# Sixteen more expert blocks multiplied ahead of the expert loop, and the first gates of it read from SBUF

## The chip, the core and the metric

The kernel runs on one core of one Trainium2 chip. The core has five engines that run beside each other, each in the order of its own queue: TensorE (PE, with the weight loads shown as PEld), VectorE (DVE), ScalarE (ACT), GpSimd (POOL) and SyncE (SP). SP issues nearly all plain DMA transfers, and POOL issues the gathers of table rows by index. The metric is the time of one execution in microseconds (us), lower is better.

## The reference

One step of a one-layer decoder for 512 prompt tokens and 64 sample tokens: a combined projection, retention, dilated attention, a mix of both, a layer norm, then a mixture of 16384 one-row experts (PEER), and a second layer norm. The change touches the experts alone:

```python
def block(xb):
    q = (xb @ w_q).reshape(PEER_BLOCK, H_PEER, 2, DK_PEER // 2)
    s = jnp.einsum('thsc,hskc->thsk', q, sub_keys).astype(jnp.float32)
    sv, si = lax.top_k(s, TOPK_PEER)
    ...
    e = i0 * N_KEYS + i1
    g = jax.nn.softmax(cv, axis=-1)
    a = jax.nn.gelu(jnp.einsum('td,thkd->thk', xb, u_tab[e]), approximate=False)
    return jnp.einsum('thk,thkd->td', (g * a).astype(xb.dtype), v_tab[e])
```

Each token picks 128 experts (8 heads of 16). An expert is a row of `peer_u` (dotted with the token, through gelu) and a row of `peer_v` (added with the weight g * a).

## The kernel before

**Two ways through the experts.** For 384 prompt tokens (TD = 3 tiles of 128) the kernel multiplies all 16384 experts densely, in 128 blocks of 128 experts, with a gate that is zero where a token did not pick an expert. For the last 128 prompt tokens and the 64 sample tokens it gathers the picked rows from memory: one indirect DMA brings one row of 1024 numbers for each of 128 partitions (a tile `row`, 512 KB), and VectorE dots it (`dot`, L1120) or adds it (`add`, L1129).

**A dense block has two parts.** `u_part(i)` (L1419) loads 512 KB of `uT` into `wraw`, splits it into a high and a low half (`whi` by ACT L1424, `wlo` by POOL L1425), makes 24 matmuls of 128x384 into a bank `tr`, and ACT's gelu makes the tile `act` (L1430). `v_part(i)` (L1558) loads 512 KB of `v`, splits it on ACT (L315) and DVE (L316), multiplies `act` by the gates to `wt` (DVE L1565), splits that into `wh` (ACT L315) and `wl` (DVE L316), and `products` makes 18 matmuls of 128x512 that add up in six banks through all 128 blocks. Both parts take their buffers from the same rings: three of `wraw`, four of `whi`, four of `wlo`, three of `wh`, four of `act`.

**The gates.** `spread(t)` (L1472) turns the picks of token tile t into gates: for each 32 tokens a tile `stage` of 128x(128x32) numbers is filled by matmuls of one-hot tiles (L1500) and copies on ACT (L1501), and stored to a DRAM tensor `gateD[b]`, 2 MB each, 12 in all (L1505). `stage` has one buffer under the tag `xh` and one under `xl`. In the loop, `gates(i)` (L1578) reads the gates of eight blocks back into a tile `gt`, in 12 DMAs of 128 KB, one from each `gateD`; its buffers are those of `stage`.

**Blocks ahead.** For blocks whose number modulo 8 is below `PG`, `u_part` runs ahead of the loop (`u_ahead`, L1435): 16 of them behind the last projection, 24 between the pieces of `spread`, the rest behind it (L1513). Their `act` goes to DRAM (`actD`, L1439), and the loop loads it back (L1592). With PG = 3 these are 48 of the 128 blocks.

**The loop** (L1585) takes block i's `act` (loaded or made by `u_part`) and then the products of block i - 1. For each block `advance` (L1139) lets some gathers through, behind a copy `pace` on POOL that waits for the block's `act`: three for a block that still has its `u_part`, 1.5 for one ahead, on average. The first step of that stream also finishes the sample tokens: `finish` (L1525) loads a tile `x1`, multiplies and adds it on POOL (L1529, L1530), makes `pz` on DVE, normalises, multiplies and adds once more, half on DVE and half on POOL (L1538, L1539), and stores the result (L1540).

**The order.** The program is not run as written: a scheduler puts the instructions of each engine in an order of its own by estimated times, and each engine then keeps to it. SP's queue is one such order too: a DMA whose buffer is not free, or whose source is not written, holds back all that SP issues after it.

Of the kernel before, what the change touches and what calls it, by code (L numbers as in the profile page):

```python
# [8 lines left out]
F32 = mybir.dt.float32  # L9
# [4 lines left out]
AF = mybir.ActivationFunctionType  # L14
# [15 lines left out]
NVEC = VEC_G[3]  # L30
DKS = 128.0 ** -0.5
MINF = -3.0e38
PG = 3
AHEAD = 1
HEAD = 16
ON_ACT = 1
# [188 lines left out]
def body(tc, I, O, dbg=None):  # L225
    nc = tc.nc
    PE, DVE, ACT, POOL, SP = nc.tensor, nc.vector, nc.scalar, nc.gpsimd, nc.sync
# [20 lines left out]
    XA = pool("xa")  # L248
# [269 lines left out]
    for g in range(NG):  # L518
        for o in range(VEC_G[g], VEC_G[g + 1], 512):
# [3 lines left out]
            t = A.tile([8, 512], F32, name="vt", tag="vt", bufs=2)  # L523
# [441 lines left out]
    G2, t = s4k("G2s"), s4k("l1s")  # L965
# [503 lines left out]
    TB = 32  # L1469
    gateD = [DR.tile([128, 128, TB], F32, name=f"gate{b}") for b in range(ND // TB)]  # L1470

    def spread(t):  # L1472
        i01 = C.tile([128, 2, 128], F32, name="i01", tag="i01", bufs=2)
        g = C.tile([128, 128], F32, name="gw", tag="gw", bufs=2)
        route(C, 8, sv[t], si[t], i01, g)
        pt = tr_ps()
        for z, x in enumerate((i01[:, 0], i01[:, 1], g)):
            PE.transpose(pt[:, 128 * z:128 * z + 128], x, ident)
        tT = C.tile([128, 4, 128], F32, name="tT", tag="tT", bufs=2)
        ACT.activation(tT[:, 0:3, :], pt[:, 0:384].rearrange("p (z t) -> p z t", z=3), AF.Copy)  # L1480
        ACT.activation(tT[:, 3, :], pt[:, 256:384], AF.Copy, scale=-1.0)
        for b in range(128 // TB):
            stage = XA.tile([128, 128, TB], F32, name="stage", tag=("xh", "xl")[b % 2], bufs=1)
            for q in range(TB // 4):
                o = TB * b + 4 * q
                oh1 = C2.tile([128, 4, 128], F32, name="oh1", tag="oh1", bufs=3)
                oh0 = C2.tile([128, 4, 128], F32, name="oh0", tag="oh0", bufs=3)
                sh = [128, 4, 128]
                DVE.tensor_tensor(oh1, iota_p[:, None, :].to_broadcast(sh), tT[:, 1, o:o + 4, None].to_broadcast(sh), op=OP.is_equal)
                ps = ac_ps()  # L1490
                for j in range(4):
                    col = lambda z: tT[:, z, o + j:o + j + 1]
                    if j < ON_ACT:

                        ACT.activation(oh0[:, j, :], iota, AF.Abs, bias=col(0), scale=-1.0)
                        ACT.activation(oh0[:, j, :], oh0[:, j, :], AF.Relu, bias=col(2), scale=col(3))
                    else:
                        E, num = (POOL, iota) if j < ON_ACT + ON_POOL[q % 2] else (DVE, iota_p)
                        E.tensor_scalar(oh0[:, j, :], num, col(0), col(2), op0=OP.is_equal, op1=OP.mult)
                    PE.matmul(ps[:, 128 * j:128 * j + 128], oh1[:, j, :], oh0[:, j, :], start=True, stop=True)  # L1500
                ACT.activation(stage[:, :, 4 * q:4 * q + 4].rearrange("p i t -> p t i"), c4(ps), AF.Copy)  # L1501
                if q % 4 == 3:
                    u_ahead(AHEAD)
                    advance(GX, stage[:, 0, :])
            SP.dma_start(gateD[128 * t // TB + b], stage)  # L1505

    u_ahead(HEAD)
    for t in range(TD):
# [69 lines left out]
    def gates(i):  # L1578
        gt = XA.tile([128, ND // TB, IG, TB], F32, name="gt", tag=("xh", "xl")[i // IG % 2], bufs=1)
        for b in range(ND // TB):  # L1580
            SP.dma_start(gt[:, b], gateD[b][:, i:i + IG, :])
        return gt

    prev, gt_next, due, last = None, gates(0), 0.0, []
    for i in range(128):  # L1585
        if i % IG == 0:
            gt = gt_next
# [48 lines left out]
```

## Time and profile before

| | before |
|---|---|
| median of 3 runs | 2478.74 us (2473.35 to 2484.56) |
| the profiled execution | 2482.92 us, of which 2480.9 us from its first to its last instruction (the span) |
| mean granted TensorE clock | 0.941 of full speed |
| busy: PE, PEld, DVE, ACT, POOL | 90%, 76%, 71%, 41%, 47% |
| expert loop, from 1580.06 to 2440.20 us | 860.14 us, PE busy 842.05 us |

Times in the trace are counted from the start of the span. A busy share is a mean over stages with different limits, so it is read by stage; `idle before <-releaser` in a row is how long the engine had waited before that instruction, and which instruction's end let it go.

### The profile page before, as it was taken

Reading aid. Unit: us, or ns where it says so; the run is one execution under the profiler, and the core shown is the slowest. Engines: PE = TensorE matmul, PEld = TensorE weight load, DVE = VectorE, ACT = ScalarE, POOL = GpSimd, SP = SyncE. Lnnn points to the kernel's source line nnn. Section 1 sums busy time; section 2 is a strip of 40 time slices with the busy share of each in tenths; the row PEclk is TensorE's granted clock in tenths of the full one; section 3 lists DMA queues with packets and bytes.
Section 4 is the critical chain, followed back from the end, with each engine's and each line's share of the span. In section 5 each row is a group of like instructions: output and inputs, shape, how many; then the busy total and the mean of one; then the engine's idle time right before and its main releaser. Section 6 shows DMA issues by size and latency. Waiting matters only on the chain.

```text
span 2480.9 us, 35644 instructions
## 1 busy us (share of the span) xinstructions
PE 2236.0 (90%) x12729; PEld 1894.0 (76%) x12729; DVE 1762.8 (71%) x3069; ACT 1006.6 (41%) x1662; POOL 1161.4 (47%) x942
## 2 busy tenths in 40 slices
PE   7899999969899996899789994899999999999995
PEld 4885666647777874899789994788888888888884
DVE  3464112355678788779999994797887888888865
ACT  2452122334455462233358893333333333333342
POOL 0022011043026545224565563677677767777742
PEclk7899999989899996999989997899999999999998
DMA  8786786476788996486767779599889989999841
GB/s 294 265 289 218 275 292 220 164 209 218 240 317 292 330 356 230 139 281 218 272 226 276 280 253 314 201 351 342 307 320 327 333 310 350 327 337 332 312 154 51
DMA packets 222494, 671.38 MB, mean 271 GB/s; under 512 B 27307, under 2 KB 80299, under 8 KB 218827
## 3 DMA queue, kind: packets, MB, share of 16 engines
q1 hardware_dynamic: 162016, 448.32, 52.5%
q0 software_dynamic: 59904, 220.62, 24.7%
q8 instruction: 100, 1.64, 0.3%
q14 instruction: 78, 0.64, 0.1%
q10 hardware_dynamic: 396, 0.16, 0.0%
HBM read 614.38 MB, written 112.40 MB: 293 GB/s over the span
## 4 chain that ended last, share of the span: by engine, by line
PE 50%; DVE 19%; DMA 15%; issue 7%; POOL 5%; ACT 3%; SPq 1%; POOLq 0%; DVEq 0%; ACTq 0%
PE mm L423 7%; PE mm L425 6%; PE mm L424 6%; PE tr L425 4%; PE tr L423 3%; PE tr L424 3%; DMA row<-in_u_dram,e 3%; PE ac L748 2%; POOL row L1111 2%; PE ac L423 2%; PE ac L424 2%; DVE ys L1129 2%; PE ac L425 2%; DVE wlo L316 2%; DMA row<-in_v_dram,e 2%
## 5 line engine op out<-in xcount | busy, mean ns | idle before, releaser
L316 DVE TENSOR_TENSOR wlo<-wraw,whi 128x1024 fp32r<-128x1024 f32 x304 | 420.3, 1387 | 259.6 <-ACT whi L315 235.4
L315 ACT ACTIVATE whi<-wraw 128x1024 fp32r<-128x1024 f32 x304 | 319.9, 1057 | 468.9 <-PE mm L424 165.4
L1425 POOL TENSOR_TENSOR wlo<-wraw,whi 128x1024 fp32r<-128x1024 f32 x128 | 331.2, 2588 | 144.5 <-ACT whi L1424 134.4
L423 PE MATMUL tr<-x,whi 128*128 128x384 f32 x1024 | 351.6, 343 | 15.7 <-ACT act L1430 13.1
L425 PE MATMUL tr<-x,wlo 128*128 128x384 f32 x1024 | 351.2, 343 | 8.4 <-POOL wlo L1425 8.2
L424 PE MATMUL tr<-x,whi 128*128 128x384 f32 x1024 | 350.3, 342 | 0.0
L1111 POOL DMA_INDIRECT row<-in_u_dram,e x192 | 253.2, 1319 | 145.4 <-DVE row L1120 111.6
L1111 POOL DMA_INDIRECT row<-in_v_dram,e x192 | 246.4, 1283 | 159.3 <-DVE y L1129 56.4
L423 PEld LDWEIGHTS tr<-x,whi 128*128 128x128 f32 x1024 | 196.5, 192 | 21.9 <-ACT act L1430 14.2
L425 PEld LDWEIGHTS tr<-x,wlo 128*128 128x128 f32 x1024 | 195.6, 191 | 10.8 <-POOL wlo L1425 9.7
L424 PEld LDWEIGHTS tr<-x,whi 128*128 128x128 f32 x1024 | 196.1, 191 | 3.6
L1129 DVE SCALAR_TENSOR_TENSOR y<-row,acts,y 128x1024 f32<-128x1024 f32 x127 | 189.3, 1490 | 12.6 <-DMA row<-in_v_dram,e 11.5
L1120 DVE SCALAR_TENSOR_TENSOR row<-row,h2g 128x1024 f32<-128x1024 f32 x128 | 172.6, 1363 | 29.5 <-DMA row<-in_u_dram,e 28.9
L1424 ACT ACTIVATE whi<-wraw 128x1024 fp32r<-128x1024 f32 x128 | 134.7, 1052 | 99.5 <-PE ac L425 31.0
L423 PE MATMUL mm<-xh,whi 128*128 128x512 f32 x384 | 154.3, 402 | 0.1
L424 PE MATMUL ac<-wlo,wh 128*128 128x512 f32 x384 | 153.9, 401 | 0.0
L423 PE MATMUL ac<-whi,wh 128*128 128x512 f32 x384 | 153.3, 402 | 0.0
L424 PE MATMUL mm<-xl,whi 128*128 128x512 f32 x384 | 152.7, 398 | 0.0
L425 PE MATMUL mm<-xh,wlo 128*128 128x512 f32 x384 | 152.3, 397 | 0.0
L315 ACT ACTIVATE wh<-wt 128x384 fp32r<-128x384 f32 x128 | 67.0, 524 | 202.2 <-DVE wt L1565 190.7
L425 PE MATMUL ac<-whi,wl 128*128 128x512 f32 x384 | 144.7, 395 | 0.0
L423 PE MATMUL mm<-whi,xh 128*128 128x256 f32 x448 | 133.1, 299 | 9.3 <-DVE gr L1359 5.4
(410 smaller groups left out, 5337.5 us busy)
## 6 DMA issues: line engine op xcount, KB each, us to landing
wraw<-in_uT_dram SPq DMA_DIRECT2D x128, 512.0 KB
wraw<-in_v_dram SPq DMA_DIRECT2D x128, 512.0 KB
out_dram<-in_cache_dram SPq DMA_DIRECT2D x64, 508.0 KB
wraw<-in_w_ada_dram SPq DMA_DIRECT2D x48, 512.0 KB
gate<-stage SPq DMA_DIRECT2D x12, 2048.0 KB
gt<-gate SPq DMA_DIRECT2D x192, 128.0 KB
kt<-in_kc_dram POOLq DMA_DIRECT2D x32, 588.0 KB
svt<-in_vc_dram SPq DMA_DIRECT2D x72, 256.0 KB
```

What stands on the lines that cost most here:

```text
L315: ACT.activation(hi, src, AF.Copy)
L316: return DVE.tensor_tensor(lo, src, fv(hi), op=OP.subtract).ins
L423: PE.matmul(ps, a[0], b[0], start=first, stop=False)
L424: PE.matmul(ps, a[0], b[1], start=False, stop=False)
L425: PE.matmul(ps, a[1], b[0], start=False, stop=last)
L748: PE.matmul(banks[bank][32 * p:32 * p + 32, a - 512 * bank:e - 512 * bank], qz[:, g, p, b2, :], kt[b2][:, a:e], start=b2 == 0, stop=b2 == 1)
L1111: POOL.indirect_dma_start(out=r, out_offset=None, in_=I[table], in_offset=bass.IndirectOffsetOnAxis(ap=e[:, j:j + 1], axis=0))
L1120: DVE.scalar_tensor_tensor(u, u, 1.0, h2, op0=OP.mult, op1=OP.mult, accum_out=a[:, j:j + 1])
L1129: DVE.scalar_tensor_tensor(y, v, a[:, j:j + 1], y, op0=OP.mult, op1=OP.add)
L1424: ACT.activation(uh, u, AF.Copy)
L1425: POOL.tensor_tensor(ul, u, fv(uh), op=OP.subtract)
```

## The change

`PG` becomes 4, so 64 blocks are multiplied ahead. The number between the pieces of `spread` stays as it was; the 16 more are issued by the `u_ahead(128)` behind the last spread tile. In the loop, 64 blocks and not 80 have a `u_part`, and 64 and not 48 load `act` from DRAM. The first eight blocks' gates of the last 32 tokens are copied by ACT from the tile `stage` that still holds them; the other eleven pieces of that first `gt` come from DRAM as before. The lines behind the change move by 2 (from L1472) or 11 (from L1584).

```diff
-PG = 3
+PG = 4
...
+    stages = {}
+
     def spread(t):
...
             SP.dma_start(gateD[128 * t // TB + b], stage)
+            stages[128 * t // TB + b] = stage
...
-    prev, gt_next, due, last = None, gates(0), 0.0, []
+    def first_gates():
+
+        gt = XA.tile([128, ND // TB, IG, TB], F32, name="gt", tag="xh", bufs=1)
+        for b in range(ND // TB - 1):
+            SP.dma_start(gt[:, b], gateD[b][:, 0:IG, :])
+        ACT.activation(gt[:, ND // TB - 1], stages[ND // TB - 1][:, 0:IG, :], AF.Copy)
+        return gt
+
+    prev, gt_next, due, last = None, first_gates(), 0.0, []
```

The order of the engines moves with it. On TensorE, between the last one-hot matmul of `spread` and the first product, there stood 35 matmuls of `u_part` (`tr<-x`) and there stand 371 now: the rest of one part and 15 whole ones, 14 parts more than before. Three other engines show what surrounds them.

POOL, from its last one-hot tile of `spread` on, before (`wlo` belongs to a `u_part`, `pace` and `row` to the gathers, `x` and `pz` to `finish`):

```order
L1499 TENSOR_SCALAR oh_13701<-kc_iota,tT 128x128
L1425 TENSOR_TENSOR wlo<-wraw,whi 128x1024
L1143 COPY pace<-act 1x1
L1111 DMA row<-in_u_dram,e_8277 128x1024
L1143 COPY pace<-act 1x1
L1111 DMA row<-in_u_dram,e_8277 128x1024 x2
L1143 COPY pace<-act 1x1
L1111 DMA row<-in_u_dram,e_8277 128x1024
L1425 TENSOR_TENSOR wlo<-wraw,whi 128x1024
```

and in the changed kernel:

```order
L1501 TENSOR_SCALAR oh_13717<-kc_iota,tT 128x128
L1425 TENSOR_TENSOR wlo<-wraw,whi 128x1024 x8
L1532 TENSOR_TENSOR x_22032<-x_22032,l1ga 128x1024
L1533 TENSOR_TENSOR x_22032<-x_22032,l1ba 128x1024
L1425 TENSOR_TENSOR wlo<-wraw,whi 128x1024 x7
L1143 COPY pace<-act 1x1
L1532 TENSOR_TENSOR x_14720<-x_14720,l1ga 64x1024
L1111 DMA row<-in_u_dram,e_8277 128x1024
```

The gathers of the last prompt tokens now begin behind fifteen `wlo`, and the first of the `x` tiles stands between the eighth and the ninth of these.

SP, a little behind the store of the last `stage`, before (`x` is for `finish`, `gate_10675` is the last of the 12 gate tensors and `gate_10664` the first; the first row of `gt` is the last piece for blocks 0 to 7, those after it are for blocks 8 to 15):

```order
L1528 DMA x_14160<-xnD 64x1024
L1528 DMA x_20745<-xnD 128x1024
L1561 DMA wraw<-in_v_dram 128x1024
L1421 DMA wraw<-in_uT_dram 128x1024
L1581 DMA gt<-gate_10675 128x256
L1581 DMA gt<-gate_10664 128x256
L1581 DMA gt<-gate_10665 128x256
```

and in the changed kernel (`gate_10680` is the first gate tensor, `act_9169` an `actD`; all `gt` rows are for blocks 8 to 15):

```order
L1531 DMA x_14720<-xnD 64x1024
L1531 DMA x_21345<-xnD 128x1024
L1421 DMA wraw<-in_uT_dram 128x1024
L1439 DMA act_9169<-act 128x384
L1421 DMA wraw<-in_uT_dram 128x1024
L1584 DMA gt<-gate_10680 128x256
L1584 DMA gt<-gate_10681 128x256
L1584 DMA gt<-gate_10682 128x256
L1439 DMA act_9170<-act 128x384
L1584 DMA gt<-gate_10683 128x256
L1584 DMA gt<-gate_10684 128x256
L1584 DMA gt<-gate_10685 128x256
```

The last piece for blocks 0 to 7 is gone from SP; loads of `uT` stand where loads of `v` stood, and the next one after these rows is behind six pieces of `gt` for blocks 8 to 15, which are still read in one go.

ACT, from the last copy of `stage` on, before:

```order
L1501 ACTIVATE stage<-ac 128x4x128
L1546 ACTIVATE yc<-ys 64x1024
L1424 ACTIVATE whi<-wraw 128x1024
L1430 ACTIVATE act<-tr 128x384
L315 ACTIVATE whi<-wraw 128x1024
L1523 ACTIVATE l1ga<-l1ga 128x1024
L1523 ACTIVATE l1ba<-l1ba 128x1024
L315 ACTIVATE wh<-wt 128x384
```

and in the changed kernel:

```order
L1503 ACTIVATE stage<-ac 128x4x128
L1549 ACTIVATE yc<-ys 64x1024
L1592 ACTIVATE gt<-stage 128x256
L1424 ACTIVATE whi<-wraw 128x1024
L1430 ACTIVATE act<-tr 128x384
L1424 ACTIVATE whi<-wraw 128x1024
L1430 ACTIVATE act<-tr 128x384
L1424 ACTIVATE whi<-wraw 128x1024
L1430 ACTIVATE act<-tr 128x384 x2
L1526 ACTIVATE l1ga<-l1ga 128x1024
L1526 ACTIVATE l1ba<-l1ba 128x1024
L1430 ACTIVATE act<-tr 128x384
```

The copy of the last gates stands right behind `stage`; the two scalings `l1ga` and `l1ba`, which wait for loads, stand in the middle of the parts ahead. In the loop itself the longest run of products on TensorE with hardly a `u_part` between them was four blocks (72 matmuls) in every eight, and is five (90) now.

## Rows read from the trace of the kernel before

**Rows 1.** The busy share of the engines over the whole span, and the granted TensorE clock in 40 equal slices (62 us each, in tenths).

```profile
PE 2236.0 (90%) x12729; PEld 1894.0 (76%) x12729; DVE 1762.8 (71%) x3069; ACT 1006.6 (41%) x1662; POOL 1161.4 (47%) x942
...
PEclk7899999989899996999989997899999999999998
```

**Rows 2.** The busy time of each engine in stretches of 100 us and in one of 10 us (columns: stretch, its length; PE, PEld, DVE, ACT, POOL busy us with their instructions; granted clock, DMA share, GB/s).

```profile
1500.00:1600.00 100.00, 58.41 (x268) 51.00 (x267) 56.54 (x62) 29.98 (x39) 51.38 (x36) 0.78 0.72 242
1600.00:1700.00 100.00, 97.12 (x465) 84.03 (x464) 85.20 (x111) 34.45 (x47) 77.45 (x59) 1.00 0.94 338
1900.00:2000.00 100.00, 99.43 (x482) 87.02 (x480) 78.89 (x91) 34.74 (x47) 70.04 (x55) 1.00 0.90 322
...
1510.00:1520.00 10.00, 0.62 (x2) 0.30 (x2) 1.22 (x1) 1.82 (x3) 6.57 (x8) 0.72 1.03 415
```

**Rows 3.** The same view for the stretch from the last one-hot matmul of `spread` to the point from which the loop runs evenly, first all instructions and then those alone that write or read a bank `tr` (the `u_part` matmuls; columns PE, PEld, DVE, ACT).

```profile
1507.80:1580.06 72.26, 30.67 (x111) 24.90 (x110) 44.21 (x44) 15.48 (x19) 38.10 (x26) 0.69 0.69 234
...
1507.80:1580.06 72.26, 8.81 (x36) 8.03 (x37) 0.00 (x0) 0.96 (x2) 0.69 0.69 234
```

**Rows 4.** TensorE's timeline in that stretch, the three matmuls that it waited longest for (start, duration, engine, line, operation, tiles, count, idle time before and releaser).

```profile
1520.27 0.69 PE L425 MATMUL tr<-x,wlo 128*128 128x384 f32 x1 [8.24 <-POOL wlo L1425]
...
1550.24 0.80 PE L423 MATMUL mm<-whi,wh 128*128 128x512 f32 x1 [23.93 <-ACT wh L315]
...
1573.79 0.79 PE L425 MATMUL mm<-whi,wl 128*128 128x512 f32 x1 [7.95 <-DVE wl L316]
```

**Rows 5.** The timelines of SP, ACT and DVE, the steps from the store of the last gates to the first `wh`.

```profile
1511.73 0.32 SPq L1505 DMA_DIRECT2D gate<-stage  x1
...
1528.76 0.33 SPq L1421 DMA_DIRECT2D wraw<-in_uT_dram  x1
1529.14 18.44 SPq L1581 DMA_DIRECT2D gt<-gate  x13
...
1528.42 1.06 ACT L1523 ACTIVATE l1ga<-l1ga 128x1024 f32<-128x1024 f32 x1 [1.15 <-DMA l1ga<-in_ln_g_dram]
1533.09 1.06 ACT L1523 ACTIVATE l1ba<-l1ba 128x1024 f32<-128x1024 f32 x1 [3.61 <-DMA l1ba<-in_ln_b_dram]
1549.66 0.52 ACT L315 ACTIVATE wh<-wt 128x384 fp32r<-128x384 f32 x1 [15.51 <-DVE wt L1565]
...
1549.10 1.00 DVE L1565 TENSOR_TENSOR wt<-act,gt 128x384 f32<-128x384 f32 x2
```

**Rows 6.** The timelines of DVE and POOL while the sample tokens are finished.

```profile
1556.04 17.23 DVE L1539 TENSOR_TENSOR pz<-pz,l2b 64x512 f32<-64x512 f32 x1
...
1556.23 1.31 POOL L1538 TENSOR_TENSOR pz<-pz,l2g 64x512 f32<-64x512 f32 x1
1557.48 2.41 POOL L1529 TENSOR_TENSOR x<-x,l1ga 128x1024 f32<-128x1024 f32 x1
1559.85 1.29 POOL L1539 TENSOR_TENSOR pz<-pz,l2b 64x512 f32<-64x512 f32 x1
1561.09 2.40 POOL L1529 TENSOR_TENSOR x<-x,l1ga 128x1024 f32<-128x1024 f32 x1
1563.45 2.39 POOL L1425 TENSOR_TENSOR wlo<-wraw,whi 128x1024 fp32r<-128x1024 f32 x1
1565.80 4.62 POOL L1530 TENSOR_TENSOR x<-x,l1ba 128x1024 f32<-128x1024 f32 x2
```

**Rows 7.** TensorE's timeline in the loop: the first matmul of a block's products, the first of the next `u_part`, the first of the next products.

```profile
2187.03 0.39 PE L423 MATMUL mm<-whi,wh 128*128 128x512 f32 x1
...
2191.22 0.33 PE L423 MATMUL tr<-x,whi 128*128 128x384 f32 x1
...
2195.41 0.40 PE L423 MATMUL mm<-whi,wh 128*128 128x512 f32 x1
```

**Rows 8.** The stretch with the longest run of parts ahead in this kernel (columns as in rows 2).

```profile
1181.00:1258.00 77.00, 63.91 (x342) 62.95 (x341) 76.76 (x255) 25.83 (x36) 46.04 (x20) 0.91 0.78 273
```

**Rows 9.** The timelines of SP and POOL: the load of the first blocks' `act`, and the copy that waited for the first of them.

```profile
1505.69 1.39 SPq L1592 DMA_DIRECT2D act<-act  x3
...
1512.25 0.17 POOL L1143 COPY pace<-act 1x1 f32<-1x1 f32 x1 [9.15 <-DMA act<-act]
```

**Rows 10.** The loop as one stretch (columns as in rows 2).

```profile
1580.06:2440.20 860.14, 842.05 (x4051) 735.83 (x4050) 696.65 (x743) 303.38 (x404) 601.91 (x450) 1.00 0.87 309
```

**Rows 11.** DMA from 1580 to 2340 us, the total, and from the page the sizes of the transfers that the loop repeats (line's tiles, queue, count, size).

```profile
DMA packets 89170, 250.03 MB, mean 329 GB/s; under 512 B 9894, under 2 KB 35257, under 8 KB 89118
...
wraw<-in_uT_dram SPq DMA_DIRECT2D x128, 512.0 KB
...
gt<-gate SPq DMA_DIRECT2D x192, 128.0 KB
...
act<-act SPq DMA_DIRECT2D x96, 192.0 KB
```

**Rows 12.** Groups of instructions by line from 1580 to 2340 us (busy us, mean ns of one | idle time before them).

```profile
L1129 DVE SCALAR_TENSOR_TENSOR y<-row,acts,y 128x1024 f32<-128x1024 f32 x123 | 184.1, 1497 | 12.6 <-DMA row<-in_v_dram,e 11.5
...
L316 DVE TENSOR_TENSOR wlo<-wraw,whi 128x1024 fp32r<-128x1024 f32 x109 | 172.4, 1581 | 38.7 <-ACT whi L315 36.9 <-issue 1.5
...
L316 DVE TENSOR_TENSOR wl<-wt,wh 128x384 fp32r<-128x384 f32 x107 | 83.7, 786 | 4.5 <-ACT wh L315 2.6 <-issue 0.6 <-PE ac L425 0.4
...
L1565 DVE TENSOR_TENSOR wt<-act,gt 128x384 f32<-128x384 f32 x108 | 65.4, 613 | 56.7 <-ACT act L1430 56.3 <-issue 0.3
```

## The prediction

> **What bounds the kernel now.** Read the busy shares and the clock slices first [rows 1]: TensorE is busy 90% of the span, and the slices show where it is not: the clock falls to 7 tenths in the 25th slice, about 1490 to 1550 us. Then the stretches of 100 us [rows 2]: from 1600 us on TensorE is busy 97% or more at full clock, with every other engine below it, so the loop runs at TensorE's pace; from 1500 to 1600 us it is busy 58%. The change works at that hole. I take its edges from the last one-hot matmul of `spread`, 1507.80, to 1580.06, from where products and `u_part` follow each other evenly [rows 3].
>
> What should the hole have cost? In the loop the products of a block take 2191.22 - 2187.03 = 4.19 us, and so does a `u_part`, 2195.41 - 2191.22 [rows 7]. A `u_part` matmul is thus 4.19 / 24 = 0.175 us, a product matmul 4.19 / 18 = 0.233. The hole holds 111 matmuls, 36 of them of `u_part` [rows 3]: 36 x 0.175 + 75 x 0.233 = 23.8 us of work in 72.3 us. **48.5 us are lost**, waits and slow clock (granted 0.69, between the levels of 1.2 and 2.4 GHz) together.
>
> Three waits make most of it [rows 4]. 8.24 us are for a `wlo` of POOL, which stood behind gathers and their `pace`, and these behind a load of `act` (issued at 1505.69, used at 1512.25 [rows 9]). 23.93 us are for the first `wh`. Its chain [rows 5]: the last gates are stored at 1511.73, SP is held until 1528.76 (17.0 us), the pieces of `gt` are issued from 1529.14 to 1547.6, `wt` starts at 1549.10, `wh` at 1549.66. The third, 7.95 us, is for a `wl` of DVE, which sat 17.23 us in one small operation while POOL ran its six operations without a break [rows 6].
>
> **What is moved.** By the order, 371 - 35 = 336 matmuls, 14 parts, go from the loop to before the first product: 14 x 4.19 = 58.7 us of work. Moved work is no gain in itself; the gain is the idle time that it fills. The two long waits need gates and DMA, and the new phase needs neither gates nor DVE, so in the ideal case all 48.5 us are saved. What the new phase loses instead:
>
> *Starved parts ahead.* By the order the halves of the next three and a half parts are there at 1507.80, because no `v` tile takes ring buffers any more. The 16 more stores of `act`, 0.2 MB each, are small beside the `uT` loads. Three holds follow. (a) On ACT a part's gelu stands behind the scaling of `l1ba`, which was there at 1533.09 [rows 5]; scaling and gelu take 1.06 + 0.5, and TensorE, with 11 left-over matmuls and five parts (1.9 + 21.0), would need that part's `tr` bank again at 1530.7: up to 4 us, none if the load comes earlier without the gathers beside it; I take 4. (b) On SP the third `uT` load stands behind six pieces of `gt`, which must wait for the 17.0 us store; thirteen such pieces took 18.44 us. After eight parts (1543) the load may be there or some 6 us late; I take 3. (c) On POOL two operations of 2.4 us stand between two `wlo`: 0 to 5, I take 2. Sum 9 us. The nearest row as a bound from above is the longest run ahead that this kernel has: 342 matmuls, 14.2 parts, in 77.0 us and not 59.7 [rows 8], 17.3 lost, so about 19 for the new phase's 15.5 parts; there the `spread` routing and the cache copies ran beside it, so I stay below it. From below it is 0, since the work itself is counted already.
>
> *To the first product.* The first `act` load is issued when the last but one part is done and SP has passed a buffer wait; it took 6.6 us from issue to use [rows 9], then `wt` and `wh` take 0.5 each [rows 5]. The last part covers 4.19. I take 3 us, from 0 to 8. The copy of the gates by ACT that replaces the last DMA piece is 128x256, half of a `wh` copy of 0.52 or so; ACT has three parts prepared ahead of it, so it costs nothing; without that cover it would be 0.5 us. The first products no longer wait for the store.
>
> *The sample tokens' finish* comes in the products as before, with POOL's run of `x`, `pz` and `wlo` shorter (three, some 6 us, not six): 2 us, from 0 to the 7.95 of now.
>
> So the hole costs 9 + 3 + 2 = 14 us (0 to 35) where it cost 48.5: 34.5 saved.
>
> **What the loop gives back.** The loop stretch has 78 parts and 121 blocks of products, 199 x 4.19 = 833.8 us in 860.1 [rows 10]: 26.3 lost, 1.74 for eight blocks. Eight blocks were 13 x 4.19 + 1.74 = 56.2 us and would be 12 x 4.19 + 1.74 = 52.0. Two things speak against that. DMA runs at 322 to 338 GB/s there [rows 2], 330 x 56.2 = 18.55 MB for eight blocks. A `uT` load (0.52 MB) goes, an `act` load (0.20) comes [rows 11], and the gathers fall from 19.5 to 18 (1.5 rows of 128x1024 numbers [rows 12], 0.79 MB): 17.44 MB, 335 GB/s at 52.0 us, the upper end of these rows. At today's 330 it would be 52.85. The other is DVE, below. I take 0.85 us for each of the 256 / 18 = 14.2 groups that have gathers: **12 us**, from 0 to 32. The gathers end at block 114 and not 105, with 14 blocks left behind them: no cost.
>
> On this the trace and the Trainium skill part. "DMA: Bandwidth & Descriptors", Specifications, gives an HBM limit of about 358 GB/s for a core; by that 17.44 MB would fit in 48.7 us, nothing would be given back, and the sum would be 2444. The rows have 415 GB/s for 10 us but never over 338 for 100 us, so I follow the rows.
>
> **The sum.** The profiled execution took 2482.92 us, 2.0 more than its span, and 4.2 more than the median of 2478.74; I take the difference off the median. 2478.7 - 48.5 + 14 + 12 = **2456 us**, 0.9% less.
>
> **The rivals.**
>
> *The loop gives nothing back* (0.17): its waits are of order and not of rate, as the 10 us row with 415 GB/s [rows 2] suggests. 2456 - 12 = 2444.
>
> *The phase ahead is starved* (0.10): it loses 19 us and not 9, as the run of [rows 8] did. For it: three engines hold the same rings. 2466.
>
> *The loop keeps DVE's waits* (0.18). DVE is busy 85.2 of 100 us [rows 2], 47.9 of 56.2, and idle 8.3, most of it in order behind `act` and `whi`. 1.5 dots less (1.497 each [rows 12]) make 45.7 us; if the 8.3 stay, eight blocks take 54.0 and not 52.0, 28 us in 14.2 groups in place of 12: 2472. Against it: waits shrink when others are early.
>
> *Five products in a row fall to DVE* (0.10), the case that is slower. For a block DVE needs `wlo` 1.581, `wt` 0.613, `wl` 0.786 and 1.5 dots of 1.497 [rows 12], 5.2 us against TensorE's 4.19. A run of four would lose 4.2 us and loses no more than 1.74 now, so prepared tiles hide the rest; a run of five, with `wh` in three buffers, loses 5.2 if nothing is hidden. That is 3.5 us more in 16 groups, 55 in place of 12: 2499. It decides from 4.7 us lost in a group on.
>
> That the change does not do what it says is shut out by the order but for one point: the first `wt` still waits for a DMA, the `act` load, which is priced above.
>
> **How the numbers follow.** The forecast has 0.45. A measurement of this kernel tells 0.5% from no change, 12.4 us: faster means below 2466.3. That takes nearly all of the forecast (0.42), the loop that gives nothing back (0.17) and a little of the starved phase (0.03): 0.62. The rest of the forecast (0.03) and of the starved phase (0.07) and most of the DVE waits (0.17) are within it: 0.27. The five in a row and the DVE case's tail are slower: 0.11. The range leaves out the slow case (0.10), the end of the hole's loss at 0 (0.05) and the DVE case's upper end (0.04): 2436 to 2482.
>
> **What would show it.** Behind the last one-hot matmul: 371 `tr` matmuls in 65 to 84 us, with waits for ACT behind `l1ba` or for `wlo` of some us; the wait before the first product below 8 us and named `wh`, with an `act` load and no gate behind it; no DVE operation of 17 us that TensorE waits for. In the loop: eight blocks in 52 to 53 us, DMA near 335 GB/s. It is wrong if eight blocks stay above 54.5 us, if the phase ahead takes over 90, or if the SP queue, held by the store, leaves TensorE without `uT` for tens of us.

## The result, and the profile after

The changed kernel took 2465.77 us (median of 7 executions, 2453.43 to 2473.57), the kernel before 2481.38 us (7 executions). The ratio is 0.994, with a 95% interval of 0.992 to 0.9959: 0.6% less, some 15 us, where 0.9% and 22.5 us were forecast. The time lies inside the range.

The page shows a little more TensorE share and the 25th clock slice at 9 tenths, where it had 7 [rows 1]. The same part of the page for the changed kernel:

```profile
PE 2237.1 (91%) x12729; PEld 1890.3 (77%) x12729; DVE 1731.6 (70%) x3069; ACT 1010.3 (41%) x1663; POOL 1157.2 (47%) x942
...
PEclk7899999978899997899989999899999999999997
```

The stretches of 100 us that answer to [rows 2] (columns as there):

```profile
1500.00:1600.00 100.00, 90.82 (x471) 85.88 (x469) 22.41 (x23) 35.99 (x49) 54.16 (x29) 0.93 0.79 257
1600.00:1700.00 100.00, 90.32 (x413) 76.38 (x413) 84.73 (x106) 34.91 (x46) 69.43 (x55) 0.97 0.84 299
1900.00:2000.00 100.00, 98.18 (x465) 84.19 (x464) 79.87 (x109) 35.69 (x47) 67.31 (x56) 1.00 0.92 334
```

TensorE's 58 us in the first became 91. The stretch behind it got worse, 90 us where 97 were busy. So the hole was filled, and part of it came back a hundred microseconds later.

To see where, I cut the end of each kernel at five events: the last one-hot matmul, the first product, the first product of the 9th block, that of the 113th, and the last product. The changed kernel by these four stretches, first all instructions, then those of the banks `tr` alone:

```profile
1503.80:1582.00 78.20, 69.04 (x375) 67.11 (x373) 8.17 (x8) 28.70 (x38) 37.35 (x18) 0.95 0.80 262
1582.00:1646.10 64.10, 56.19 (x238) 47.02 (x239) 55.72 (x66) 20.94 (x27) 50.96 (x38) 0.91 0.74 261
1646.10:2328.60 682.50, 662.68 (x3123) 567.86 (x3122) 556.04 (x640) 237.38 (x315) 459.57 (x368) 1.00 0.92 330
2328.60:2439.00 110.40, 104.45 (x479) 88.69 (x478) 100.28 (x88) 36.95 (x48) 76.37 (x53) 0.97 0.67 239
...
1503.80:1582.00 78.20, 69.04 (x373) 67.11 (x373) 0.00 (x0) 7.66 (x16) 0.95 0.80 262
1582.00:1646.10 64.10, 17.21 (x94) 16.67 (x94) 0.00 (x0) 1.91 (x4) 0.91 0.74 261
1646.10:2328.60 682.50, 230.10 (x1250) 219.16 (x1250) 0.00 (x0) 25.54 (x52) 1.00 0.92 330
2328.60:2439.00 110.40, 34.98 (x192) 33.19 (x190) 0.00 (x0) 3.86 (x8) 0.97 0.67 239
```

And the kernel before by the same events:

```profile
1507.80:1550.20 42.40, 8.80 (x38) 7.84 (x36) 16.37 (x22) 7.44 (x9) 16.80 (x14) 0.66 0.98 336
1550.20:1610.90 60.70, 51.77 (x218) 43.39 (x219) 47.10 (x50) 20.40 (x27) 39.75 (x29) 0.87 0.58 197
1610.90:2342.50 731.60, 715.70 (x3434) 624.24 (x3432) 616.11 (x661) 253.06 (x339) 543.12 (x406) 1.00 0.92 330
2342.50:2452.60 110.10, 108.86 (x525) 95.24 (x526) 67.22 (x66) 40.27 (x53) 40.85 (x30) 1.00 0.41 135
```

With the prediction's prices (4.19 / 24 us for a matmul of a part, 4.19 / 18 for one of a product) the first eight blocks of the changed kernel hold 94 x 4.19 / 24 + 144 x 4.19 / 18 = 49.9 us of work in 64.1: 14.2 are lost, to waits and to the lower clock together. So for each stretch, and for the runs below (lost us; the last column is the time behind the last product; ratio to the kernel before, with its 95% interval):

| kernel | ratio | to the first product | first eight blocks | blocks 9 to 112 | last sixteen | behind |
|---|---|---|---|---|---|---|
| before | 1 | 36.5 | 14.3 | 23.4 | 1.8 | 28.3 |
| after | 0.994 (0.992 to 0.9959) | 13.3 | 14.2 | 28.5 | 10.4 | 28.6 |
| e1_gates_dram | 0.993 (0.9904 to 0.9955) | 8.8 | 13.2 | 24.5 | 7.9 | 28.6 |
| e2_copy_only | 1.0069 (1.0045 to 1.0094) | 4.1 | 33.5 | 48.0 | 3.8 | 28.3 |
| e3_no_x | 0.9886 (0.9856 to 0.9916) | 9.3 | 7.6 | 21.0 | 1.2 | 28.3 |
| e4_finish_early | 0.9952 (0.9931 to 0.9972) | 23.7 | 6.7 | 21.6 | 6.0 | 28.8 |
| e5_x_dve | 0.9876 (0.9852 to 0.9899) | 12.1 | 5.0 | 29.3 | 1.5 | 28.3 |
| e6_own_ring | 1.0573 (1.0546 to 1.0599) | 4.3 | 19.1 | 160.4 | 32.6 | 35.9 |
| e7_pg5 | 1.0134 (1.0108 to 1.016) | 10.7 | 12.7 | 41.3 | 6.5 | 60.0 |
| e8_rate | 0.9925 (0.9902 to 0.9948) | 9.5 | 10.7 | 23.5 | 2.0 | 36.3 |
| e9_uhi_two | 0.9932 (0.9907 to 0.9957) | 10.3 | 3.0 | 42.4 | 1.9 | 37.8 |
| e10_gather_ahead | 0.9941 (0.9921 to 0.996) | 27.4 | 10.6 | 18.0 | 0.6 | 28.3 |
| e11_before_x_dve | 0.9961 (0.9944 to 0.9978) | 38.5 | 6.4 | 20.7 | 0.1 | 28.3 |
| e12_rows_ahead | 0.9969 (0.9955 to 0.9983) | 22.2 | 4.9 | 36.8 | 0.1 | 28.6 |

Each row is one profiled execution. Five kernels whose loop is the same (after, e1, e3, e4, e5) show 21.0 to 29.3 in blocks 9 to 112, so a difference of a few us in that column says little. Each edit also lets the scheduler put all engines in a new order, so a row is never the edit alone.

**The stretch ahead** lost what was forecast. In both kernels eleven pieces of the first gates are issued ahead of the store of the last ones; the twelfth, which SP issued at 1529.14 before [rows 5], is now ScalarE's copy. The store (issued at 1505.13) still holds SP, for 3.9 us at a load of `x`. `uT` goes out at 1518.02, and ScalarE can split it at 1530.80 (SP's waits from 1503 to 1524, total us, times, longest; timelines of SP and ScalarE; then TensorE's waits from 1503 to 1582 and the first product in its timeline):

```profile
SPq L1531 <- DMA gate<-stage: 3.9, 1, 3.9
...
1511.49 4.77 SPq L1531 DMA_DIRECT2D x<-xnD  x2
1518.02 0.34 SPq L1421 DMA_DIRECT2D wraw<-in_uT_dram  x1
...
1530.80 1.06 ACT L1424 ACTIVATE whi<-wraw 128x1024 fp32r<-128x1024 f32 x1 [4.90 <-DMA wraw<-in_uT_dram]
...
PE tr L425 <- POOL wlo L1425: 3.1, 2, 1.7
PE tr L423 <- ACT act L1430: 2.2, 2, 1.5
PE tr L423 <- ACT whi L1424: 1.0, 1, 1.0
...
1582.02 0.79 PE L423 MATMUL mm<-whi,wh 128*128 128x512 f32 x1 [2.78 <-ACT wh L315]
```

**The first eight blocks** lost as much as before. No operation takes 17.23 us any more [rows 6], but the finish is still there, cut in pieces (timelines of VectorE, GpSimd and TensorE):

```profile
1615.77 6.04 DVE L1568 TENSOR_TENSOR wt<-act,gt 128x384 f32<-128x384 f32 x1 [1.16 <-ACT act L1430]
...
1615.44 2.40 POOL L1533 TENSOR_TENSOR x<-x,l1ba 128x1024 f32<-128x1024 f32 x1
1617.79 1.29 POOL L1541 TENSOR_TENSOR pz<-pz,l2g 64x512 f32<-64x512 f32 x1
1619.04 2.34 POOL L1425 TENSOR_TENSOR wlo<-wraw,whi 128x1024 fp32r<-128x1024 f32 x1
...
1622.41 0.50 PE L423 MATMUL mm<-whi,wh 128*128 128x512 f32 x1 [2.96 <-ACT wh L315]
```

The gates' product `wt`, 0.55 us alone, begins just behind GpSimd's first operation and ends at 1621.81, when GpSimd's run of three (1615.44 to 1621.38) is over. `wh` and the product stand behind it. Another wait of this kind came at 1611.28 (1.40). The longest is not of this kind: the 3.21 us at 1639.06, before the eighth block's products. Its `wt`, at 1637.90, took 0.55 us, stood behind splits and products of gathered rows on VectorE, and had no tensor operation of GpSimd beside it. At the same block e1, e3 and e5 wait 3.40, 2.98 and 2.62 us, and e8, with fewer rows to a block, 0.17 (these runs are described below). With a wait of 0.33 us these make 7.9 of the 14.2 us; the rest is the clock (0.91 granted).

**The last sixteen blocks** show the same thing with the finish of the gathered prompt tokens (same views):

```profile
2419.47 2.40 POOL L1532 TENSOR_TENSOR x<-x,l1ga 128x1024 f32<-128x1024 f32 x1 [6.78 <-DMA x<-xnD]
...
2422.95 2.36 POOL L1533 TENSOR_TENSOR x<-x,l1ba 128x1024 f32<-128x1024 f32 x1
2425.27 1.25 POOL L1541 TENSOR_TENSOR pz<-pz,l2g 128x512 f32<-128x512 f32 x1
...
2422.87 4.07 DVE L1568 TENSOR_TENSOR wt<-act,gt 128x384 f32<-128x384 f32 x1
...
2427.55 0.80 PE L423 MATMUL mm<-whi,wh 128*128 128x512 f32 x1 [3.39 <-ACT wh L315]
```

**The loop** has a new, regular wait: about 1.2 us in 9 of 13 groups of eight blocks, where a part's high half comes late after ScalarE waited for the end of products, which hold the ring's buffers (TensorE's waits from 1655 to 2320 us; then ScalarE and TensorE in one group):

```profile
PE tr L423 <- ACT whi L1424: 10.8, 9, 1.2
PE mm L423 <- ACT wh L315: 3.6, 6, 1.0
...
1907.14 1.06 ACT L1424 ACTIVATE whi<-wraw 128x1024 fp32r<-128x1024 f32 x1 [3.14 <-PE ac L425]
...
1908.24 0.45 PE L423 MATMUL tr<-x,whi 128*128 128x384 f32 x1 [1.19 <-ACT whi L1424]
```

### The profile page after: what moved, and what is told of

It is laid out like the page before. It is cut to its first block, busy times and chain, and to the rows that moved or that the text cites. A ratio compares the mean times of both kernels' runs of the same rounds, so it can differ in the third digit from the quotient of the medians.

```text
span 2467.7 us, 35754 instructions
## 1 busy us (share of the span) xinstructions
PE 2237.1 (91%) x12729; PEld 1890.3 (77%) x12729; DVE 1731.6 (70%) x3069; ACT 1010.3 (41%) x1663; POOL 1157.2 (47%) x942
## 4 chain that ended last, share of the span: by engine, by line
PE 54%; DVE 19%; DMA 15%; issue 5%; POOL 3%; ACT 3%; SPq 1%; POOLq 0%; DVEq 0%; ACTq 0%
PE mm L423 7%; PE mm L425 7%; PE mm L424 7%; PE tr L425 4%; PE tr L423 4%; PE tr L424 4%; DVE wlo L316 3%; PE ac L1502 3%; PE ac L748 3%; PE ac L425 2%; PE ac L423 2%; PE ac L424 2%; DVE ys L1129 2%; DMA row<-in_v_dram,e 2%; DMA act<-act 2%
## 5 line engine op out<-in xcount | busy, mean ns | idle before, releaser
L316 DVE TENSOR_TENSOR wlo<-wraw,whi 128x1024 fp32r<-128x1024 f32 x304 | 396.0, 1308 | 316.5 <-ACT whi L315 287.3
L1425 POOL TENSOR_TENSOR wlo<-wraw,whi 128x1024 fp32r<-128x1024 f32 x128 | 321.9, 2517 | 148.1 <-ACT whi L1424 141.4
L1111 POOL DMA_INDIRECT row<-in_u_dram,e x192 | 242.7, 1264 | 147.6 <-DVE row L1120 117.7
L1129 DVE SCALAR_TENSOR_TENSOR y<-row,acts,y 128x1024 f32<-128x1024 f32 x127 | 192.1, 1513 | 14.3 <-DMA row<-in_v_dram,e 13.0
L1424 ACT ACTIVATE whi<-wraw 128x1024 fp32r<-128x1024 f32 x128 | 135.0, 1054 | 129.5 <-DMA wraw<-in_uT_dram 38.5
L1120 DVE SCALAR_TENSOR_TENSOR row<-row,h2g 128x1024 f32<-128x1024 f32 x128 | 177.2, 1402 | 10.5 <-DMA row<-in_u_dram,e 10.4
L425 PE MATMUL ac<-whi,wl 128*128 128x512 f32 x384 | 139.4, 395 | 0.0
```

The source lines that it names most:

```text
L316: return DVE.tensor_tensor(lo, src, fv(hi), op=OP.subtract).ins
L425: PE.matmul(ps, a[1], b[0], start=False, stop=last)
L1111: POOL.indirect_dma_start(out=r, out_offset=None, in_=I[table], in_offset=bass.IndirectOffsetOnAxis(ap=e[:, j:j + 1], axis=0))
L1120: DVE.scalar_tensor_tensor(u, u, 1.0, h2, op0=OP.mult, op1=OP.mult, accum_out=a[:, j:j + 1])
L1129: DVE.scalar_tensor_tensor(y, v, a[:, j:j + 1], y, op0=OP.mult, op1=OP.add)
L1424: ACT.activation(uh, u, AF.Copy)
```

## The experiments

My first theory after the result: the hole's 36.5 us became 13.3 as forecast, and the rest of the forecast gain went into the finish on GpSimd, at both ends of the loop. The rivals: ScalarE's copy of the gates costs or gives something of its own; the place of the finish and not its work is at fault; the loop loses by its ring or its DMA.

**The two parts of the change apart.** e1 is the changed kernel with the gates from DRAM, e2 has the copy without the 16 blocks:

```diff
-    prev, gt_next, due, last = None, first_gates(), 0.0, []
+    prev, gt_next, due, last = None, gates(0), 0.0, []      # e1
-PG = 4
+PG = 3                                                      # e2
```

> PG = 4, but the first eight blocks' gates all come from DRAM again. If the 14 parts moved ahead cover the store of the last gates and its read (the first product of the changed kernel starts 78 us behind the last one-hot matmul, the store is over within some 20 us), the ACT copy is worth nothing: ratio to the kernel before 0.994, first product within 3 us of 1582 us, as with the copy. If the copy is what the change lives on, 8 us or more are lost again: 0.997 or above, and the first product waits for a wt that waits for a gate DMA.

> PG = 3, with the ACT copy of the first gates. If the 23.9 us wait of the kernel before was for the store and its read back alone, the first product comes some 20 us earlier and the ratio is 0.992 or below, as good as the whole change. If the rest of the start (the DMA traffic of those us, the finish of the sample tokens on POOL, DVE and SP) is late next, it stays above 0.996: the wait moves and is not removed.

e1 took 2461.28 us, ratio 0.993: the copy gives nothing that can be measured once 15 parts stand between the store and the first product. e2 took 2493.87 us, ratio 1.0069: slower. Its first product comes 6 us behind the last one-hot matmul, so the copy alone does close the hole, but the finish then falls beside the loop's own parts. TensorE's longest wait there, and what stood ahead of that `wlo` in GpSimd's queue:

```profile
1576.67 0.69 PE L425 MATMUL tr<-x,wlo 128*128 128x384 f32 x1 [12.35 <-POOL wlo L1425]
...
1556.92 5.51 POOL L1542 TENSOR_TENSOR pz<-pz,l2b 64x512 f32<-64x512 f32 x1
...
1562.53 2.36 POOL L1532 TENSOR_TENSOR x<-x,l1ga 128x1024 f32<-128x1024 f32 x1
1565.05 5.71 POOL L1111 DMA_INDIRECT row<-in_u_dram,e  x1 [0.16 <-issue]
1570.78 2.35 POOL L1533 TENSOR_TENSOR x<-x,l1ba 128x1024 f32<-128x1024 f32 x1
```

Blocks 9 to 112 of e2 lose 48.0 us too, with 16 waits for `wlo` (11.8 us from 1655 to 2320) of which the kernel before has none. Why that loop loses so much more is open.

**The finish.** e3 leaves out GpSimd's two operations on the residual, e4 writes the sample tokens' finish ahead of the 24 parts, e5 moves the two operations to VectorE:

```diff
-        POOL.tensor_tensor(x, x, l1ga[0:P], op=OP.mult)   # e3: both lines out
-        POOL.tensor_tensor(x, x, l1ba[0:P], op=OP.add)
+        DVE.tensor_tensor(x, x, l1ga[0:P], op=OP.mult)    # e5
+        DVE.tensor_tensor(x, x, l1ba[0:P], op=OP.add)
...
-    u_ahead(128)                # e4: behind the sample tokens' finish() instead
```

> The changed kernel without POOL's two operations on x in finish (the residual enters unscaled, part of the result is left out). The first eight blocks' products lose 14.2 us in the changed kernel. If POOL's multiplies and adds beside DVE's wt, and the store of pz that waits for both, make that loss, it falls to 6 us or less and the ratio to 0.990 or 0.991. If it is the restart of the gathers and of the rings, it stays at 12 us or more, ratio 0.993 or 0.994.

> The changed kernel with the finish of the sample tokens put ahead of the last 24 parts in the program, so that it runs while DVE is nearly idle (9.8 us busy of 84.7 in the phase ahead). If the finish makes the 14.2 us of the first eight blocks, they lose 6 us or less and the ratio is 0.990 or 0.991, with a few us more in the phase ahead, where POOL's operations stand between the wlo. If the loss is the restart, 0.994 as before.

> The changed kernel with the two operations of the finish that scale the residual (x times l1ga, x plus l1ba, in the sample tokens' finish and in the four others) on VectorE in place of GpSimd. On GpSimd the two took 5.28 us and about 2.4 us of a 64x1024 and 128x1024 tile, and VectorE's gate products beside them took 2.7 to 6.0 us where the same product takes 0.55 alone. Theory 1 (GpSimd's chain of operations is what starves the first eight blocks and holds VectorE's products): about 1.2 us for each on VectorE, 2.4 in all beside each finish; the first eight blocks lose 6 to 8 us as in the run without the two operations, the last sixteen 1 to 4, and the time falls to a ratio of about 0.989 to 0.991 of the kernel before. Theory 2 (it is the amount of work beside the first blocks, on whichever engine): the two on VectorE hold its gate products as long, the first eight blocks lose 12 to 15 us, and the ratio stays at 0.993 to 0.996.

e3 took 2450.33 us, e4 2465.08, e5 2449.10. Without the two operations the first eight blocks lose 7.6 and the last sixteen 1.2. Moving the finish ahead only moves its cost: the first eight blocks gain 7.5, the stretch ahead loses 10.4 more. On VectorE the same work leaves 5.0 and 1.5 us lost. e5 by the four stretches:

```profile
1509.20:1586.30 77.10, 67.89 (x377) 65.99 (x375) 28.71 (x25) 32.28 (x42) 37.05 (x16) 0.98 0.84 275
1586.30:1641.20 54.90, 52.14 (x239) 44.52 (x240) 44.69 (x57) 17.35 (x24) 38.27 (x34) 0.97 0.84 285
1641.20:2324.50 683.30, 662.33 (x3124) 568.35 (x3122) 564.76 (x643) 236.83 (x314) 465.82 (x374) 1.00 0.92 332
2324.50:2426.00 101.50, 100.34 (x478) 86.99 (x478) 84.87 (x87) 36.80 (x48) 57.29 (x43) 1.00 0.69 247
```

Some of these operations moved as well: four of the five `x` products with `l1ga` begin by 1553.0 on VectorE, which has little to do in the stretch ahead; on GpSimd they began at 1543.0, 1581.4, 1602.8, 2335.7 and 2419.5. Engine and place are not told apart by e5; the earlier place alone, in e4, gained nothing. e5 is the version that beats both kernels (its row of the table is an execution of 2456.41 us).

e11 puts the same edit into the kernel before:

> The kernel before with only the two operations that scale the residual in the finish on VectorE in place of GpSimd. If the finish on GpSimd is a cost of its own beside the change: the first eight blocks lose about 5 us in place of 14.3, the hole at the gates stays at 36 us, the time is 9 us shorter, a ratio of about 0.996, and the change then brings 21 us (2.5 us more than the 15 it brought here, since the last gathered tokens' finish in the last sixteen blocks costs nothing either). If the two only cost something together with the sixteen blocks ahead: a ratio of 0.999 or above.

It took 2471.18 us, ratio 0.9961 as expected: the first eight blocks lose 6.4 in place of 14.3, the hole stays at 38.5. So the finish on GpSimd cost some 9 us before the change too (4 more or less, from the interval). With it out of the way the change brings 0.9876 / 0.9961 = 0.9915, 21 us (some 7 us more or less, from both intervals), close to the 22.5 that were forecast for it.

**The loop's ring.** e6 gives the loop's parts one buffer of their own for each half, e9 (on e5) two for the high halves alone; `x1` has a buffer less in both:

```diff
-        uh = w_hi().rearrange("p (k e) -> p k e", e=128)
+        uh = (w_hi() if own is None else own()).rearrange("p (k e) -> p k e", e=128)   # e9; e6 has it for ul too
...
-            a = u_part(i)
+            a = u_part(i, own)
...
```

> The changed kernel with one buffer each of its own (uhi, ulo) for the split weights of the first halves that are multiplied inside the loop, in place of the four-buffer rings that the gathered tokens' weights share (a buffer less for x1 makes room). In the loop of the changed kernel TensorE loses about 1.36 us ten times, once in each group of eight blocks, where a first half of the loop waits for its high part, after ScalarE waited for a free buffer of that ring during the run of five second halves. Ring theory: those waits go, the loop of 112 blocks loses 14 to 19 us in place of 28.5, and the ratio falls to about 0.989 to 0.990. Rival (the high part is late because its weights' DMA or ScalarE's own queue is late; the ring only shows it, and with one own buffer the wait moves to the buffer's release): the loop loses 25 us or more and the ratio stays at 0.992 to 0.996.

> The kernel of e5_x_dve, with a ring of two buffers of its own (uhi) for the high parts of the first halves multiplied inside the loop; their low parts stay in the shared ring, and x1 has two buffers in place of three. In e5_x_dve TensorE loses 13.1 us in 11 waits for such a high part, and the run with one own buffer each for both parts gained nothing and lost 132 us in blocks 9 to 112, since the next first half could not be split before the one ahead was multiplied. Ring theory: with two buffers the high part is ready before the run of five second halves ends, the 11 waits go, and blocks 9 to 112 lose 14 to 19 us in place of 29.3; the ratio falls to 0.982 to 0.984. Rival (the wait is for ScalarE's place in the order, or any ring of fewer than four buffers holds the split back): blocks 9 to 112 lose 29 us or more, and the ratio is 0.987 or above.

e6 took 2622.68 us. One buffer is held until the part is multiplied, and ScalarE, which works in order, stands still with the `wh` of the next products behind it (ScalarE's waits in e6, 1655 to 2320 us; in the changed kernel its waits for the end of TensorE's products before a part's split come to 28.6):

```profile
ACT uhi L1424 <- PE tr L424: 92.9, 19, 7.4
```

e9 took 2468.09 us, slower than e5. TensorE's waits in e9, 1655 to 2320 us:

```profile
PE mm L423 <- ACT wh L315: 11.7, 10, 1.4
PE mm L425 <- DVE wl L316: 8.7, 8, 1.9
PE tr L423 <- ACT uhi L1424: 0.3, 1, 0.3
```

The ring was what that wait hung on: 11.9 us of it in e5 became 0.3. But the loop lost 42.4 us and not 29.3, since 20.4 us of waits for `wh` and `wl` stand there where e5 has 6.7, and 37.8 us follow the last product where e5 has 28.3. The ring theory named the wait rightly and its worth wrongly; the buffer that `x1` gave up is not told apart from it.

**The amount of work ahead, and the pace.** e7 multiplies 80 blocks ahead, e8 lowers the pace of the gathered steps:

```diff
-PG = 4
+PG = 5          # e7
-RATE = 3.0
+RATE = 2.75     # e8
```

> The changed kernel with five of each eight blocks multiplied ahead (80 blocks) in place of four (64): sixteen more behind the last spread tile, four loops' worth of first halves fewer in each group. The sixteen move 67 us of product time (16 times 4.19) from the loop to the phase ahead, so nothing of that is gained by itself. Theory of the filled hole (the gain of the change was the gates' hole of 36 us, which is full with 64, so nothing is left to fill): the phase ahead has 67 us more of work and loses about as much at its end as now, the loop has less time per group for its gathered rows, at about 47 us a group and 8 x 1.05 MB of second halves plus 3 x 1.05 MB of first halves plus the same gathered rows; the ratio comes out at 0.994 to 1.010. Rival (moving still more out of the loop relieves it): below 0.990.

> The changed kernel with the pace of the gathered tokens' steps in the loop set from 3.0 to 2.75. The loop gave back 14 us (5 in blocks 9 to 112 and 8.6 in the last sixteen, where the last gathered tokens' finish now falls into the last blocks). Theory 1 (the loop's shorter groups meet VectorE's and DMA's work per block; a slower pace lowers that per block and moves its end further back): blocks 9 to 112 lose less than 28.5 us by up to 5, the last sixteen lose more than 10.4 or work is left behind the loop; together the ratio is 0.993 to 1.000. Theory 2 (the waits are a matter of the order in a group and not of the load): the losses of blocks 9 to 112 stay at 26 to 31 us and the rest gets longer by 5 us or more, the ratio 0.996 to 1.002.

e7 took 2511.78 us, slower than before by 1.3%, a little outside what I expected. The stretch ahead fills as well as with 64 (10.7 lost), so nothing is left to gain there; the loss is behind. From the code, the pace gives the loop 80 x 1.5 + 48 x 3 = 264 steps in place of 288, and the gathered tokens are not done when the products are (100 us of e7's loop; its last products, and what follows):

```profile
2100.00:2200.00 100.00, 99.39 (x463) 84.59 (x461) 83.18 (x85) 34.98 (x47) 70.33 (x55) 1.00 0.95 349
...
2352.00:2450.00 98.00, 92.35 (x431) 78.36 (x430) 87.60 (x77) 31.93 (x42) 72.79 (x54) 1.00 0.83 298
2450.00:2511.00 61.00, 0.97 (x5) 0.44 (x3) 41.97 (x54) 5.66 (x8) 24.73 (x17) 0.54 0.32 117
```

e8 has 264 steps as well and took 2459.68 us, which its interval does not tell from after: the last sixteen blocks lose 2.0, not 10.4, but 36.3 us follow the last product. The finish left the blocks and came back behind them.

**Rows gathered in the stretch ahead.** e10 is e5 with half a gathered step for each of the 24 parts; e12 is e10 with GpSimd's pace copy on every second part, tied to an older activation, and with the sample tokens' finish held back into the loop (e10's edit to the parts ahead):

```diff
-    u_ahead(128)
...
+    for i in pre:
+        a = u_part(i)
+        copy_old(CU, SP.dma_start(actD[i], a).ins)
+        due += 0.5
+        advance(int(due), a, steps)
+        due -= int(due)
```

> The kernel of e5_x_dve, with half a gathered step for each of the last 24 first halves multiplied ahead (12 of the 288 steps that the loop paces), so that gathered rows are loaded and multiplied in the stretch in which VectorE was busy for 9.8 of 84.7 us and the DMA moved 262 GB/s, and no longer in the loop, which stands at 330 GB/s. The sample tokens' finish falls into that stretch with them. DMA theory (the loop's remaining losses come from its rate): the first eight blocks lose 3 to 5 us, blocks 9 to 112 lose less than 29.3, by up to 5, the steps end 4 blocks earlier, and the ratio is 0.983 to 0.987. Rival (the finish and the rows ahead hold ScalarE, GpSimd and SP, which the first halves need for their split and their loads): the stretch ahead loses 17 us or more in place of 12.1, the loop gives nothing back, and the ratio is 0.988 to 0.992.

> The kernel of e10_gather_ahead with two of its costs taken out: GpSimd's pace copy in the stretch ahead comes only for every second first half and waits for the activation of two first halves earlier (in e10_gather_ahead it waited for the newest one, and the next low parts stood behind it on GpSimd: TensorE lost 6.40 us at 1567.31 to a low part), and the sample tokens' finish is held back to the 40th of the pasted tokens' 256 steps, in the loop, by a copy from that block's activation. Theory 1 (e10_gather_ahead lost its gain to GpSimd's order and to the finish, not to the rows): the stretch ahead loses 12 us or less in place of 27.4, the first eight blocks 3 to 7 in place of 10.6, blocks 9 to 112 about 18 to 24, since the finish now costs a few there; the ratio is 0.982 to 0.986, below e5_x_dve. Theory 2 (the rows themselves hold the loads and the splits of the first halves): the stretch ahead loses 18 us or more, and the ratio is 0.987 to 0.992.

Neither gained: 2467.35 and 2468.75 us, slower than e5 (the profiled execution of e12 took 2460.33). The stretch ahead loses 27.4 and 22.2 us in place of 12.1. In e10 one wait of it is a `wlo` that stood behind the finish and the pace copies on GpSimd:

```profile
1567.31 0.69 PE L425 MATMUL tr<-x,wlo 128*128 128x384 f32 x1 [6.24 <-POOL wlo L1425]
```

e12 took that cause away and still lost 10 us more than e5 there, as its second theory said. Whether the rows, their loads or the pace copies that stayed cost this is not shown, and the ratio lies above the range of either theory. What the rows bring in blocks 9 to 112 is unclear: 18.0 us lost in e10, 36.8 in e12 with the same rows ahead and the finish in it.

## Why the prediction was right, and which term was wrong

- *The hole's loss, and the stretch ahead*: right in sum. 9 + 3 us were forecast up to the first product, 13.3 measured. Of the three holds, (a), 4 us behind `l1ba`, did not come: the gelu behind it was over at 1525.90, before TensorE waited. (b), taken at 3 for a late `uT`, cost 3.7: at 1532.29 (1.48) and 1547.88 (0.77) TensorE waited for a gelu, at 1534.34 (1.43) for a `wlo`, and each stood behind a split whose `uT` load had landed late. (c), the two operations on GpSimd, cost 1.7 where I took 2. Then 1.0 went on a split at 1578.62 and 2.8 before the first product; the rest is the clock (0.95 granted).
- *The chain of the first `wh`*: misread in part; of the sum only the 3 us of (b) leaned on it. The 17.0 us of SP were not one hold by the store: SP issued seven loads in them, and waited longest (5.3) for VectorE's split of a `v` tile to free a buffer, and 2.8 for the store. Nor did VectorE wait for a gate when it came to the first `wt`: that began without a gap behind two statistics of the finish. So the finish may have had a share in the 23.93 us; how large is not shown (SP's waits in the kernel before, 1511 to 1530 us; VectorE's timeline just ahead of the `wt` at 1549.10 [rows 5]):

```profile
SPq L1421 <- DVE wlo L316: 5.3, 1, 5.3
SPq L1421 <- DMA gate<-stage: 2.8, 1, 2.8
...
1547.90 1.27 DVE L843 BATCH_NORM_STATS2 lst<-pz 64x6 f32<-64x512 f32 x2
```

- *The sample tokens' finish, 2 us*: this is the step that failed. The prediction read the 17.23 us operation of [rows 6] as what the finish costs, and three operations in place of six as the cure (the unbroken run beside it was of eight, 1556.23 to 1572.72). Behind 1580.06, where its hole ended, 2.3 us more were lost before, so 4.3 were to be lost in the first eight blocks; 14.2 were, as many as before the change. The run became several of three and less, and these still held work of VectorE that TensorE then waited for (2.96 and 1.40 us). e3, e5 and e11 show it: take GpSimd's two operations away and 6.6 to 9.2 us go, with or without the change.
- *The gathers' end, "no cost"*: failed as well. The last row was added at 2409.2 us, in the 125th block, and not in the 114th. The same count put the end at block 105 in the kernel before, whose trace has it at 2349.2, in the 114th, so the count was some nine blocks early there already. The finish behind it met the last blocks and 10.4 us were lost where 1.8 had been. e5 shows that it was GpSimd's work and not the place: there the last row is added at 2396.7, in the 124th block, and 1.5 us are lost.
- *The loop gives back 12 us*: right in size by luck, 5.1 in blocks 9 to 112 and 8.6 in the last sixteen, since the second part is the finish. Eight blocks took 682.5 / 13 = 52.5 us (52.85 forecast) at 330 GB/s. The Trainium skill, "DMA: Bandwidth & Descriptors", Specifications, with its 358 GB/s for a core, would have had nothing given back. The 100 us stretches of this loop from 1500 us on reach 334 at most, but e7's loop reached 349 from 2100 to 2200, so the 338 of the rows was no upper end. That the rate set the 5.1 us is not shown: the waits named are of order (`whi`, `wh`), and the spread of that column is larger (21.0 to 29.3).
- *The sum*: in the spans, -50.8 + 13.3 + 14.2 + 5.1 + 8.6 = -9.6 us, and -4.0 us by which the last one-hot matmul comes earlier (in the runs here it lies anywhere from 1498 to 1515 us, so this is scatter), and 0.3 behind: -13.3, beside the spans' 2480.9 and 2467.7.
- *The rivals*: five products in a row did not fall to VectorE, and the loop did not keep DVE's waits (eight blocks in 52.5 us, not 54.0). Whether its blocks 9 to 112 gave something or nothing back is not decided by 5.1 us. The stretch ahead was not starved: the time measured is that rival's 2466, but by chance, since the stretch lost 13.3 us. None of them had the finish in it, and it was the finish that took the gain.

VectorE and GpSimd held each other in these rows: a `wt` of 0.55 us took 6.04 beside GpSimd's three operations. The Trainium skill, "SBUF — State Buffer", section "SBUF: two separate sides", tells this as a lock: of a VectorE operation with two inputs in SBUF and a GpSimd operation that reads SBUF, the one that starts first has the shared pair of ports for its whole instruction, and the other fully blocks. The rows agree and go on: `wt` waited not for one instruction but for a run of three (2.40, 1.29 and 2.34 us).

What stays open: why e2's loop loses twice as much; what sets the 20 to 30 us of blocks 9 to 112; what makes the wait before the eighth block's products; and why blocks 9 to 112 lose 18.0 us with the rows ahead in e10 and 36.8 in e12.

## What to carry to other kernels

When a hole is filled with work that needs none of the engines that were late, the late engines' own work comes next: price it again where it will now fall, at its new neighbours, and not by the one longest wait that it shows today. A chain of small operations on GpSimd held VectorE here for the length of its unbroken run (6.04 us, and 17.23 before), and TensorE waited behind; try the other engine first, at a time when that one is idle (here two lines of code, some 16 us). And a pace tuned for one order of the work is part of that order: with the loop shortened, see where its last step lands.

## What the hardware showed that I had not expected

A VectorE operation can be held through several GpSimd operations in a row: 0.55 us became 6.04 here, and in e10 a row's product of 1.22 us took 8.18 beside a run of three `wlo`. The other way is there too: GpSimd's `x` product, 2.4 us alone, took 5.28 at 1602.81 beside VectorE's own run (e5's expectation reads this as the time of a tile of 64x1024; that one took 2.36). And a lower clock came where waits had come close together: after the 3.21 us at 1639.06 the granted clock was 0.74 in the 10 us from 1640, with TensorE busy in all of them. It had been busy 8.2, 7.3 and 6.8 us of the three stretches of 10 us before:

```profile
1640.00:1650.00 10.00, 10.00 (x35) 7.91 (x34) 8.73 (x13) 2.41 (x4) 7.74 (x7) 0.74 1.05 410
```

In e5 the wait of 2.62 us at 1636.90 stood alone (TensorE busy 10.0 and 7.2 us of the 10 us from 1620 and from 1630), and the clock stayed at 1.00 in the 10 us from 1640. Its first eight blocks had a granted clock of 0.97 where the changed kernel had 0.91.
